# Input projection by a seven-product 2x2 block scheme, in two passes over the tokens

## The chip, the cores and the metric

One core of one Trainium2 chip runs the whole program. The metric is device time in microseconds (us) for one execution. All tensors are 32-bit floats. TensorE multiplies a stationary operand (128x128, loaded just before) by a moving operand of up to 512 columns and adds into PSUM; VectorE (DVE), ScalarE (ACT) and GpSimd (POOL) do the rest, and DMA queues are fed from SP and ACT.

## The reference

One layer of an encoder trunk. `x` is 2048 tokens by 1024 features, `w_in` is 1024 by 4616, `mem` is 256 memory tokens.

```python
h = rmsnorm(x, norm_g)
proj = h @ w_in
qk_raw, v, o, z_a, gates, u, z_b, qc, z_c = jnp.split(proj, _OFFS, axis=-1)
# widths 1024, 512, 512, 512, 8, 512, 512, 512, 512
y_a = mlstm_branch(qk_raw, v, o, ig, fg, ...) * silu(z_a)   # conv of 4 taps + silu on qk, then chunked recurrence
y_b = pool_branch(u, pool_w, pool_scale) * silu(z_b)        # causal means over 2, 4, 8, 16 tokens
y_c = mem_attn_branch(qc, mem, ...) * silu(z_c)             # softmax attention to 256 memory tokens
x = x + concatenate([y_a, y_b, y_c]) @ w_out
return rmsnorm(x, final_norm_g)
```

## The kernel before

Every large product is made from a high part and a low part of each operand (`hi` is the value rounded to the matmul's input format, `lo` the rest), and `mm3` issues three matmuls: hi by hi, hi by lo, lo by hi. The high part is made by an ACT copy, the low part by a subtraction on DVE or POOL.

**Input.** `load_x` reads the transposed `x` in four blocks of 512 tokens and eight slices of 128 features, multiplies by the norm's gain, splits into high and low (`x` tiles, one for each block and slice, all resident), and adds up squares on POOL (`acc`). The row norm is not applied to `x`: its factor (`rt`, broadcast as `rbc`) is applied to each product when it is taken out of PSUM. So the first products start before any norm is known.

**Projection, channel layout.** For a tile of 128 channels and a block of 512 tokens, `proj` issues 8 slices by 3 matmuls with the weights stationary and 512 token columns moving. There are 24 such channel tiles: 8 for q and k (`evac_qk` takes each out, applies the four-tap convolution by one ACT and three DVE instructions, then silu, then stores to `d_qk`), 4 for `zc`, 4 for `qc`, 4 for `zb` and 4 for `u`. The `u` weights are first multiplied by the pooling matrix (`pool_w`, the matmuls of L478).

**Projection, token layout.** v, o, z_a and the gates are made with the `x` tiles stationary and 256 weight columns moving (264 in the one group that holds the eight gate columns): 6 groups by 16 token tiles by 8 slices by 3 matmuls. Results go to `d_tok`. The memory's keys and values are made in the same stage and stay in SBUF.

**Order.** q and k; token layout with `gate_stats`; attention, head by head (`attend`: scores, softmax, transposes, product with values); pooling; then the last stage, in which each chunk of 128 tokens runs the recurrence (`cell`) and the output projection (`out_k`, 12 slices by 3 by 2 matmuls of 512 columns). The steps of `attend` are queued by `later(n, fn)` and run by `tick()` between projections. The output weights are prepared during the last pooling products (`prep_wo`).

A scheduler that works ahead of time orders the instructions of every engine by program order among those it holds to be ready, and sets the waits. Tile pools hand their space on: a tile of a later pool waits for the earlier tiles at its address.

## Time and profile before

| | |
|---|---|
| Runs, us | 1280.02, 1276.82, 1281.62 (median 1280.02) |
| Span of the profiled execution | 1275.6 us |
| TensorE matmul busy | 1243.3 us (97%) |
| TensorE weight load busy | 1086.5 us (85%) |
| VectorE busy | 582.6 us (46%) |
| ScalarE busy | 399.4 us (31%) |
| GpSimd busy | 247.6 us (19%) |
| DMA | 124.52 MB, mean 98 GB/s |

The span runs from the first to the last instruction of one profiled execution; what lies around it is the difference to the runs (4.4 us to the median). Matmuls overlap each other in the array, so "busy" counts time with at least one in flight, and the distance from one start to the next tells the rate. PE is the matmul, PEld its weight load.

### The profile page before, as it was taken

The numbers are of one execution on the slowest core, as the hardware profiler recorded it, in microseconds if no ns is written. First come the engines' busy times: TensorE is split into PE (matmuls) and PEld (weight loads), VectorE is DVE, ScalarE is ACT, GpSimd is POOL, SyncE is SP. The second block draws the span as 40 slices with busy tenths as digits, with TensorE's granted clock in tenths as the row PEclk, the third lists the DMA queues.
The fourth block names the chain that finished last, engine by engine and source line by source line (L and its number), as shares of the span: only waits on it lengthen the run. The fifth ranks groups of instructions, "written<-read, shape, count | busy, mean of one in ns | idle before, by whom it ended". The sixth has DMA issues, their size and how long they took to land. (4 is left out here: it accounts for less than half of the span.)

```text
span 1275.6 us, 17705 instructions
## 1 busy us (share of the span) xinstructions
PE 1243.3 (97%) x7063; PEld 1086.5 (85%) x7063; DVE 582.6 (46%) x1123; ACT 399.4 (31%) x832; POOL 247.6 (19%) x202
## 2 busy tenths in 40 slices
PE   6889999999999999999999999999989999999997
PEld 5667888999999999888888888888878888888886
DVE  6987766223300000163636354235445665656434
ACT  6744333223331221152535240100244222222212
POOL 4633000000000010000000004212434332323110
PEclk9999999999999999999999999999989999999999
DMA  6423323133311221011111012111496545454511
GB/s 208 137 62 108 100 67 104 63 102 106 96 61 67 79 70 56 26 33 33 34 33 42 25 30 62 43 49 49 158 291 236 172 150 174 149 183 140 184 57 66
DMA packets 87202, 124.52 MB, mean 98 GB/s; under 512 B 6352, under 2 KB 60880, under 8 KB 87120
## 3 DMA queue, kind: packets, MB, share of 16 engines
q1 hardware_dynamic: 56400, 102.42, 24.7%
q10 hardware_dynamic: 30720, 20.98, 5.2%
q8 instruction: 55, 0.90, 0.3%
q14 instruction: 27, 0.22, 0.0%
HBM read 85.56 MB, written 37.81 MB: 97 GB/s over the span
## 5 line engine op out<-in xcount | busy, mean ns | idle before, releaser
L147 PE MATMUL mm<-x,whi 128*128 128x512 f32 x720 | 283.9, 395 | 10.1 <-ACT x L214 7.1
L148 PE MATMUL mm<-x,whi 128*128 128x512 f32 x720 | 282.1, 392 | 2.4 <-DVE x L215 2.4
L149 PE MATMUL mm<-x,wlo 128*128 128x512 f32 x720 | 282.5, 392 | 0.0
L147 PE MATMUL mm<-whi,x 128*128 128x256 f32 (+1 forms) x768 | 217.8, 284 | 0.0
L149 PE MATMUL mm<-whi,x 128*128 128x256 f32 (+1 forms) x768 | 217.1, 283 | 0.0
L148 PE MATMUL mm<-wlo,x 128*128 128x256 f32 (+1 forms) x768 | 216.9, 282 | 0.0
L147 PEld LDWEIGHTS mm<-x,whi 128*128 128x128 f32 x720 | 136.1, 189 | 38.9 <-ACT x L214 7.1
L138 POOL TENSOR_TENSOR wlo<-wraw,whi 128x1024 fp32r<-128x1024 f32 (+1 forms) x23 | 55.7, 2421 | 557.8 <-ACT whi L137 492.1
L148 PEld LDWEIGHTS mm<-x,whi 128*128 128x128 f32 x720 | 136.0, 189 | 32.0 <-DVE x L215 3.8
L149 PEld LDWEIGHTS mm<-x,wlo 128*128 128x128 f32 x720 | 135.8, 189 | 29.0 <-issue 0.2
L147 PEld LDWEIGHTS mm<-whi,x 128*128 128x128 f32 x768 | 146.2, 190 | 0.4
L148 PEld LDWEIGHTS mm<-wlo,x 128*128 128x128 f32 x768 | 146.2, 190 | 0.2
L149 PEld LDWEIGHTS mm<-whi,x 128*128 128x128 f32 x768 | 146.0, 190 | 0.0
L442 ACT ACTIVATE tev<-mm,rt 128x256 f32<-128x256 f32 x96 | 45.4, 474 | 169.9 <-PE mm L149 168.8
L198 DVE SCALAR_TENSOR_TENSOR cacc<-text,col,cacc 128x512 f32<-128x512 f32 x96 | 82.1, 874 | 11.5 <-ACT cacc L196 10.1
L618 PE MATMUL mm<-woh,ybh 128*128 128x512 f32 x192 | 73.1, 404 | 0.0
L618 PE MATMUL mm<-wol,ybh 128*128 128x512 f32 x192 | 72.0, 398 | 0.0
L618 PE MATMUL mm<-woh,ybl 128*128 128x512 f32 x192 | 70.0, 393 | 0.0
L502 DVE TENSOR_TENSOR zc<-mm,rbc 128x512 f32<-128x512 f32 x16 | 11.0, 690 | 121.0 <-PE mm L149 121.0
L137 ACT ACTIVATE whi<-wraw 128x1024 fp32r<-128x1024 f32 (+1 forms) x37 | 39.3, 1062 | 81.5 <-PE mm L148 35.7
L774 DVE SCALAR_TENSOR_TENSOR hh<-hh,ss,gz 128x128 f32<-128x128 f32 x64 | 50.0, 841 | 30.4 <-POOL ss L772 30.4
L138 DVE TENSOR_TENSOR wlo<-wraw,whi 128x1024 fp32r<-128x1024 f32 (+1 forms) x14 | 17.2, 1228 | 94.0 <-ACT whi L137 94.0
(245 smaller groups left out, 1974.1 us busy)
## 6 DMA issues: line engine op xcount, KB each, us to landing
d_t<-tev ACTq DMA_DIRECT2D x96, 128.0 KB, 1.7
wraw<-in_wch_dram SPq DMA_DIRECT2D x17, 512.0 KB, 3.6
xr<-in_xT_dram SPq DMA_DIRECT2D x32, 256.0 KB, 3.4
d_qk<-cacc ACTq DMA_DIRECT2D x32, 256.0 KB, 2.6
d_y<-y SPq DMA_DIRECT2D x32, 256.0 KB, 2.6
yr<-d_y SPq DMA_DIRECT2D x16, 512.0 KB, 4.6
qk<-d_qk SPq DMA_DIRECT2D x16, 512.0 KB, 4.0
gz<-d_t SPq DMA_DIRECT2D x16, 512.0 KB, 3.8
```

The costliest lines, as they stand in the source:

```text
L137: A.activation(hi, raw, AF.Copy)
L138: lo_eng.tensor_tensor(lo, raw, r32(hi), ALU.subtract)
L147: T.matmul(po, ah, bh, start=first, stop=False)
L148: T.matmul(po, ah, bl, start=False, stop=False)
L149: T.matmul(po, al, bh, start=False, stop=last)
L198: V.scalar_tensor_tensor(c, t[:, i:i + BW], w(i), c, ALU.mult, ALU.add)
L442: A.activation(ev, pp[:, :256], (AF.Copy, AF.Sigmoid, AF.Silu)[n // 2], scale=rt[:, t:t + 1])
L502: V.tensor_tensor(z, pp, rbc[:, blk(b)], ALU.mult)
L618: T.matmul(outs[c][n], l, w[:, n * 512:(n + 1) * 512], start=i == 0 and p_ == 0, stop=i == KO - 1 and p_ == 2)
L774: V.scalar_tensor_tensor(hh[:, h], hh[:, h], ss[:, h:h + 1], gz[:, 1, h], ALU.mult, ALU.mult)
```

## The change

The product of tokens by features by channels is cut in two along each of the three, and the eight block products become seven by additions before and after (four sums of the token blocks S1 to S4, four of the weight blocks T1 to T3 and N4, seven additions of results). Token halves are two blocks of 512, feature halves four slices each, channel halves two tiles of 128 (or two groups of 256 in token layout). One such "quad" makes two channel tiles for 1024 tokens, or 512 token-layout columns for 1024 tokens. All 1024 tokens' seven forms of `x` fill the space that all of `x` filled before, so the kernel makes two passes `s` over halves of the tokens, and every weight is loaded and split in each pass.

The sums must be of normalised rows, so rows are normalised before the split. In the first pass squares are summed before anything else (`load_y_raw`, `norm_cols`, `scale_y`); for the second, `row_norms` squares whole rows during the first pass. Memory keys and values are made at the very start and kept in DRAM (`d_km`, `d_vm`). The eight gate columns get products of their own (`gates`). The order is: tok0, tok1, gates, 4 q/k quads, 4 attention quads, 4 pooling quads, tok2 (during which the second pass's forms replace the first's, one by one), then tok0, tok1, tok2, gates, `gate_stats`, q/k, attention, pooling, and the last stage as before. The preparation of output weights stands behind the last pooling quad.

```diff
+CH_ORDER = (("A11", "B11", "P", True), ("S2", "T2", "U", True), ("A12", "B21", "P", False),
+            ("S1", "T1", "V", True), ("S3", "T3", "W", True), ("S4", "B22", "V", False), ("A22", "N4", "W", False))
+TOK_ORDER = (("A11", "B11", "P", True), ("A12", "B21", "P", False), ("S2", "T2", "U", True),
+             ("S1", "T1", "V", True), ("S3", "T3", "W", True), ("S4", "B22", "V", False), ("A22", "N4", "W", False))
...
-            return ps.tile(list(shape), F32, name=tag, tag=tag, bufs={"mm": 3, "pv": 1}.get(tag, 2))
+            return ps.tile(list(shape), F32, name=tag, tag=tag, bufs={"mm": 4}.get(tag, 2))
...
+        def load_y_raw(s, y, i, sq=None):
...
+                    dma(y[i][h][k], xT[4 * h + k, :, b * BW:(b + 1) * BW])
...
+                            A.activation(q, y[i][h][k], AF.Square)
+                            G.tensor_tensor(acc[:, i], acc[:, i], q, ALU.add)
+        def scale_y(s, y, i):
+            b = 2 * s + i
+            rb = bcast(rt[:, 4 * b:4 * b + 4], 4)
...
+                    V.scalar_tensor_tensor(y[i][h][k], y[i][h][k], g, rb, ALU.mult, ALU.mult)
+        def x_split(f, srcs):
+            fi = FORMS.index(f)
...
+                t = xp.tile([P, 2, BW], F32R, name=f"x{f}_{k}", tag=f"x{4 * fi + k}")
+                A.activation(t[:, 0], srcs[k], AF.Copy)
+                lo_engine(3).tensor_tensor(t[:, 1], srcs[k], r32(t[:, 0]), ALU.subtract)
+        def x_steps(y):
...
+            def each(out, x0, x1, op):
+                for k in range(4):
+                    G.tensor_tensor(out[k], x0[k], x1[k], op)
+            return {
+                "A11": lambda: x_split("A11", a),
+                "A12": lambda: x_split("A12", b_),
+                "pre": lambda: each(e, c, d, ALU.add),
+                "S2": lambda: (each(c, a, c, ALU.subtract), each(a, e, a, ALU.subtract), x_split("S2", a)),
+                "S1": lambda: x_split("S1", e),
+                "S3": lambda: x_split("S3", c),
+                "S4": lambda: (each(b_, b_, a, ALU.subtract), x_split("S4", b_)),
+                "A22": lambda: x_split("A22", d),
+            }
+        NWF = 8
...
+            def prep(self, f):
+                B = self.raw
+                share = {"qk": 2, "tok": 3}.get(self.kind, 2)
+                if f == "T2":
+                    G.tensor_tensor(B["B11"], B["B12"], B["B11"], ALU.subtract)
+                    B["T1"] = B["B11"]
...
+                    G.tensor_tensor(t2, B["B22"], B["T1"], ALU.subtract)
...
+                if f == "T3":
+                    G.tensor_tensor(B["B12"], B["B22"], B["B12"], ALU.subtract)
...
+                if f == "N4":
+                    G.tensor_tensor(B["B21"], B["B21"], B["T2"], ALU.subtract)
...
+                    t = wb.tile([P, 2, 4, P], F32R, name="wf", tag="wf", bufs=NWF)
+                    A.activation(t[:, 0], src, AF.Copy)
+                    lo_engine(share).tensor_tensor(t[:, 1], src, r32(t[:, 0]), ALU.subtract)
+        def run_ch(q, d11, d12, d21, d22, done):
...
+            for n, (xfm, wfm, acc, opens) in enumerate(q.order):
+                if opens:
+                    banks[acc] = bank([P, BW], "mm")
+                pp = banks[acc]
+                for k in range(4):
+                    wh, wl = q.forms[wfm][k]
+                    mm3(pp, wh, wl, xf[xfm][k][:, 0], xf[xfm][k][:, 1], opens and k == 0, k == 3)
+                if n == 0:
+                    s1 = ev("s1")
+                    A.activation(s1, pp, AF.Copy)
+                elif n == 1:
+                    u2 = ev("u2")
+                    V.tensor_tensor(u2, pp, s1, ALU.add)
...
+        def run_tok(q, step=None):
...
+                for bk in range(2):
+                    pp = banks[acc][bk]
+                    for r in range(2):
+                        sl = slice((2 * bk + r) * P, (2 * bk + r + 1) * P)
+                        for k in range(4):
+                            mm3(pp[:, r], xt[:, 0, sl], xt[:, 1, sl], wh, wl, opens and k == 0 and r == 0, k == 3,
+                                pin=opens and k == 0 and r == 1)
...
+        def gates(s):
...
+                for k in range(4):
+                    w = wt[:, (k0 + k) * 16:(k0 + k) * 16 + P]
+                    T.matmul(pp, w, xf[f][k][:, 0], start=first and k == 0, stop=False, skip_group_check=True)
+                    T.matmul(pp, w, xf[f][k][:, 1], start=False, stop=last and k == 3, skip_group_check=True)
+            prod(g1, "A11", wgp, 0, True, True)
+            prod(g2, "S3", wgn, 0, True, False)
+            prod(g1, "A12", wgp, 4, False, True)
+            prod(g2, "A22", wgp, 4, False, True)
...
+        def conv(q):
+            s = q.s
+            ts = [misc([P, 3 + 2 * BW], "text", bufs=3) for _ in range(2)]
...
+                for i in (2, 1, 0):
+                    V.scalar_tensor_tensor(c, t[:, i:i + 2 * BW], w(i), c, ALU.mult, ALU.add)
...
+        y = make_y(1)
+        load_y_raw(1, y, 0)
+        load_y_raw(1, y, 1)
+        xs = x_steps(y)
...
+        run_tok(next(it), turn)
...
+        close(wcm)
+        fcm, fp = pool("fp")
...
+        for i in range(8):
+            prep_wo(i)
+        ybs[0] = load_y(0)
```

In `load_y_raw` the blocks `a`, `b_`, `c`, `d` of `x_steps` are token half 0 with feature halves 0 and 1, then token half 1 with feature halves 0 and 1.

## Rows read from the trace of the kernel before

**Rows 1.** The profile's page, its first lines: span, and busy time by engine.

```profile
span 1275.6 us, 17705 instructions
...
PE 1243.3 (97%) x7063; PEld 1086.5 (85%) x7063; DVE 582.6 (46%) x1123; ACT 399.4 (31%) x832; POOL 247.6 (19%) x202
```

**Rows 2.** TensorE matmuls by line and shape: count | busy us, mean ns of one | idle before.

```profile
L147 PE MATMUL mm<-x,whi 128*128 128x512 f32 x720 | 283.9, 395 | 10.1 <-ACT x L214 7.1 <-DVE text L192 2.9
...
L147 PE MATMUL mm<-whi,x 128*128 128x256 f32 x640 | 181.5, 284 | 0.0
...
L147 PE MATMUL mm<-whi,x 128*128 128x264 f32 x128 | 36.3, 284 | 0.0
...
L147 PE MATMUL pt<-x,whi 128*128 128x512 f32 x32 | 13.2, 414 | 0.0
...
L478 PE MATMUL aux<-pwr,wraw 128*128 128x128 f32 x64 | 8.4, 274 | 0.0
...
L147 PE MATMUL pv<-x,whi 128*128 128x512 f32 x16 | 6.4, 399 | 0.0
```

**Rows 3.** TensorE's timeline at 800 us: start us, duration us, what.

```profile
800.66 0.39 PE L147 MATMUL mm<-x,whi 128*128 128x512 f32 x1
...
805.19 0.39 PE L149 MATMUL mm<-x,wlo 128*128 128x512 f32 x1
805.42 1.05 PE L478 MATMUL aux<-pwr,wraw 128*128 128x128 f32 x8
806.23 0.48 PE L147 MATMUL mm<-x,whi 128*128 128x512 f32 x1
```

**Rows 4.** TensorE's timeline at 400 us, in the token-layout stage.

```profile
399.78 0.28 PE L147 MATMUL mm<-whi,x 128*128 128x256 f32 x1
...
402.99 0.28 PE L147 MATMUL mm<-whi,x 128*128 128x256 f32 x1
```

**Rows 5.** TensorE's timeline: first matmul of the program, and of the token-layout stage.

```profile
7.13 0.79 PE L147 MATMUL mm<-x,whi 128*128 128x512 f32 x1 [7.13 <-ACT x L214]
...
210.88 0.28 PE L147 MATMUL mm<-whi,x 128*128 128x256 f32 x1
```

**Rows 6.** Busy time of each engine in three stretches, then granted clock, DMA share, GB/s.

```profile
128.00:160.00 32.00, 32.00 (x143) 26.50 (x142) 25.51 (x47) 11.51 (x16) 2.39 (x1) 1.00 0.34 99
544.00:576.00 32.00, 32.00 (x177) 27.83 (x176) 22.70 (x52) 17.95 (x44) 2.38 (x1) 1.00 0.11 33
944.00:952.00 8.00, 6.74 (x25) 5.94 (x26) 1.29 (x2) 3.21 (x6) 4.68 (x3) 0.59 1.01 318
```

**Rows 7.** VectorE's timeline in the pooling stage.

```profile
787.90 1.58 DVE L510 TENSOR_TENSOR y<-p,zb 128x512 f32<-128x512 f32 x1
...
793.21 0.68 DVE L510 TENSOR_TENSOR y<-p,zb 128x512 f32<-128x512 f32 x1
```

**Rows 8.** GpSimd's timeline in the same stretch.

```profile
787.88 1.06 POOL L642 TENSOR_TENSOR usum<-uext 128x526 f32<-128x526 f32 x1
```

**Rows 9.** VectorE instructions by line and shape.

```profile
L583 DVE TENSOR_TENSOR tl<-pt,th 128x512 fp32r<-128x512 f32 x32 | 22.0, 687 | 10.0 <-ACT th L582 10.0
...
L820 DVE SCALAR_TENSOR_TENSOR xo<-xo,fs,gfb 128x1024 f32<-128x1024 f32 x15 | 20.1, 1340 | 10.2 <-POOL fs L813 10.2
```

**Rows 10.** GpSimd instructions by line and shape.

```profile
L138 POOL TENSOR_TENSOR wlo<-wraw,whi 128x1024 fp32r<-128x1024 f32 x22 | 53.2, 2418 | 516.2 <-ACT whi L137 450.4 <-PE mm L149 65.8
L221 POOL TENSOR_TENSOR acc<-acc,sq 128x512 f32<-128x512 f32 x28 | 40.4, 1443 | 28.4 <-ACT sq L220 22.0 <-ACT acc L217 5.3 <-DMA wraw<-in_wch_dram 0.3
...
L642 POOL TENSOR_TENSOR usum<-usum 128x512 f32<-128x512 f32 x4 | 4.2, 1040 | 2.8 <-DVE usum L642 2.8
```

**Rows 11.** GpSimd's timeline at the start of the program.

```profile
9.33 1.32 POOL L221 TENSOR_TENSOR acc<-acc,sq 128x512 f32<-128x512 f32 x1 [7.68 <-ACT sq L220]
...
38.63 1.47 POOL L154 TENSOR_TENSOR rt<-ms,mhalf 128x4 f32<-128x4 f32 x1 [0.70 <-DVE ms L153]
```

**Rows 12.** The DMA queues between 8 and 16 us: packets and bytes.

```profile
DMA packets 1475, 2.68 MB, mean 335 GB/s; under 512 B 297, under 2 KB 297, under 8 KB 1475
```

More of the change, by code (lines that the diff above doesn't have):

```diff
@@ L141, in load_w, with xslot @@
[L141 to L149 removed]
+        def xslot(i, shape, name, dtype=F32):
+            return xp.tile(shape, dtype, name=name, tag=f"x{i}")
@@ L151, in rsqrt_mean, with mm3 @@
+        def mm3(po, ah, al, bh, bl, first, last, pin=False):
+            ins = T.matmul(po, ah, bh, start=first, stop=False, skip_group_check=True)
+            if pin:
+                tc.keep_in_program_order(ins)
+            T.matmul(po, ah, bl, start=False, stop=False, skip_group_check=True)
+            T.matmul(po, al, bh, start=False, stop=last, skip_group_check=True)
         def rsqrt_mean(dst, src, w, n):
@@ new lines, in hybrid_block, with load_upto @@
+        quads = []
+        for s in range(2):
+            seq = [("tok", 0), ("tok", 1)]
+            rest = [(n, i) for n in ("qk", "att") for i in range(4)] + [("pool", i) for i in (3, 2, 1, 0)]
+            seq = seq + rest + [("tok", 2)] if s == 0 else seq + [("tok", 2)] + rest
+            quads += [Quad(n, s, i) for n, i in seq]
+        stream = [(q, f[1]) for q in quads for f in q.order]
+        state = {"next": 0, "used": 0, "loaded": 0}
+        def load_upto(q):
+            while state["loaded"] <= quads.index(q):
+                quads[state["loaded"]].load()
+                state["loaded"] += 1
@@ new lines, in pump, with used @@
+        def pump():
+            while state["next"] < len(stream):
+                q, f = stream[state["next"]]
+                if state["used"] + q.cost > NWF:
+                    return
+                load_upto(q)
+                q.prep(f)
+                state["used"] += q.cost
+                state["next"] += 1
+                n = quads.index(q) + 1
+                if n < len(quads) and f == ("N4" if q.tok else "T3"):
+                    load_upto(quads[n])
+        def used(q):
+            state["used"] -= q.cost
+            pump()
@@ L358, in gate_stats, with row_norms @@
+        def row_norms(t):
+            xr = misc([P, D], "xnr")
+            dma(xr, xn[t * P:(t + 1) * P])
+            A.activation(xr, xr, AF.Square, accum_out=ssq[:, t:t + 1])
+        for i in range(4):
+            conv(next(it))
+            for t in (2 * i, 2 * i + 1):
+                row_norms(8 + t)
+        rsqrt_mean(rt[:, 8:16], ssq[:, 8:16], 8, D)
+        tick()
+        close(mcm)
         def gate_stats():
@@ new lines, in attention_stage @@
+        def attention_stage():
+            mcm, pools["m"] = pool("m2")
+            set_evac(1, 1, 1)
+            ks = {}
+            kmhl = misc([P, 2, H, NMEM], "kmhl", F32R)
+            vmhl = misc([P, 2, MT, GW], "vmhl", F32R)
+            dma(r32(kmhl), d_km)
+            dma(r32(vmhl), d_vm)
+            kv["kmh"], kv["kml"], kv["vmh"], kv["vml"] = kmhl[:, 0], kmhl[:, 1], vmhl[:, 0], vmhl[:, 1]
+            for _ in range(4):
+                attention(next(it))
+            flush()
+            close(mcm)
@@ new lines, in pooling_stage, with turn @@
+        def pooling_stage():
+            mcm, pools["m"] = pool("m3")
+            set_evac(2, 2, 1)
+            for _ in range(4):
+                pooling(next(it))
+            flush()
+            close(mcm)
+        kv = {}
+        attention_stage()
+        pooling_stage()
+        mcm, pools["m"] = pool("m4")
+        set_evac(2, 2, 2)
+        y = make_y(1)
+        load_y_raw(1, y, 0)
+        load_y_raw(1, y, 1)
+        xs = x_steps(y)
+        old = dict(xf)
+        new = {}
+        def turn(n):
+            if n == 0:
+                scale_y(1, y, 0)
+                scale_y(1, y, 1)
+                xs["pre"]()
+            else:
+                f = TOK_ORDER[n - 1][0]
+                xf.clear()
+                xs[f]()
+                new.update(xf)
+                xf.clear()
+                xf.update(old)
@@ new lines, in hybrid_block @@
+        run_tok(next(it), turn)
+        xs["A22"]()
+        new["A22"] = xf["A22"]
+        xf.update(new)
+        run_tok(next(it))
+        flush()
+        close(mcm)
+        mcm, pools["m"] = pool("m5")
+        set_evac(2, 2, 4)
+        run_tok(next(it))
+        later(2, gates(1))
+        run_tok(next(it))
+        gate_stats()
+        for _ in range(4):
+            conv(next(it))
+        flush()
+        close(mcm)
+        attention_stage()
+        pooling_stage()
+        close(wcm)
@@ L838, in hybrid_block @@
             if c + 1 < NT:
-                outs[c + 1] = [bank([P, 512], "pv" if n and c % 2 == 0 else "mm") for n in range(2)]
+                outs[c + 1] = [bank([P, 512], "mm") for n in range(2)]
                 for i in range(8):
@@ L860, in hybrid_block @@
         close(scm)
+        close(fcm)
         close(xcm)
```

770 lines of the change are left out of this document (397 added, 373 removed).

## Prediction

> **What bounds the kernel now.** I read the page's head first: matmuls are in flight 1243.3 of 1275.6 us, while DVE, ACT and POOL are busy 46, 31 and 19% [rows 1]. A busy PE need not be PE at its peak, so I looked next at its timeline for the distance between starts. In the channel layout 20 steps take 805.19 - 800.66 = 4.53 us, 0.2265 us a matmul [rows 3]; in the token layout 27 steps take 402.99 - 399.78 = 3.21 us, 0.1189 us [rows 4]. The reader should see that these are steady and that no wait stands between them: time is the number of matmuls by these two prices, plus what is lost at the start and at the change to the last stage. The start: the first matmul is at 7.13 us and the token stage begins at 210.88 [rows 5]. In between lie 768 projection matmuls, 174.0 us, and about 8 us of small ones for the norms (an estimate: four broadcasts and four column sums, about 1 us each), so 210.9 - 182 = 29 us are lost. At the change to the last stage PE idles and its granted clock falls to 0.59 in the stretch 944 to 952 us [rows 6].
>
> **What it removes.** The line L147 is the first of `mm3`'s three matmuls. It has 720 + 32 + 16 = 768 entries of 512 columns and 640 + 128 = 768 in token layout [rows 2], so 2304 matmuls of each kind. After: 12 channel quads by 2 passes by 7 products by 4 slices by 3 = 2016, and 3 token quads by 2 by 7 by 16 by 3 = 2016. That is 288 fewer of each: -288 x 0.2265 = -65.2 us and -288 x 0.1189 = -34.2 us.
>
> **What it adds on TensorE.** Gates: 32 matmuls of 512 columns a pass, 64 x 0.2265 = +14.5 us, which before were 8 extra columns of 128 triples with the mean of the 256-wide ones, 284 ns [rows 2]. Turning the gates to token rows takes 8 small products a pass (two blocks of four token tiles), each issued as two instructions as those of L478 are: 32 in all, at that line's step (806.23 - 805.42)/8 = 0.10 us [rows 3], +3.2. The `u` weights are multiplied once more: 64 more of L478 [rows 2], +6.4. Norm sums, broadcasts, memory keys and values stay in number. Net on PE: -65.2 - 34.2 + 14.5 + 3.2 + 6.4 = **-75.3 us**.
>
> **Work that moves to the other engines.** Here I chose what to believe. Each channel quad now has seven weight forms to split (seven ACT copies, seven subtractions, half on DVE and half on POOL) and four weight sums on POOL: 7.5 POOL instructions of 512 columns. DVE gets five additions out of PSUM, 3.5 subtractions and, for q/k, six convolution steps of 1024 columns. With 0.69 and 1.34 us [rows 9] that is 8.5 x 0.69 + 6 x 1.34 = 13.9 us, against 84 x 0.2265 = 19.0 us of PE. Alone it fits. But DVE and POOL get in each other's way: a two-source DVE instruction took 0.68 us alone and 1.58 us beside one POOL instruction of 1.06 us that began 20 ns earlier [rows 7, 8]: 0.90 us for each meeting. If all 7.5 meet, a q/k quad costs DVE 13.9 + 6.7 = 20.6 us, 1.6 more than PE; if they fall on the additions out of PSUM, nothing. Eight such quads: 0 to +13; I take **+6**, nearer the middle because just over half of DVE's work there has two sources in SBUF.
>
> The Trainium skill has a rule that speaks against this change ("SBUF — State Buffer", section "Who interferes with whom"): a DVE instruction with two SBUF inputs and a GpSimd instruction that reads SBUF exclude each other, and the second waits for all of the first. The rows agree that it waits, at 0.90 us of 1.06; by the rule's letter the sum would be some 10 us longer.
>
> Attention quads are longer on PE by two `attend`s, and DVE was busy 22.7 of 32 us in the densest attention stretch and 25.5 of 32 in q/k [rows 6]; with the lighter evacuation I leave attention and pooling at nothing, covered by PE. If that cover is gone in pooling too, see the slow rival. ACT has 12 us in a quad of 19, and the second reading of the weights (some 18 MB, with 4 MB for `row_norms`) spreads over a millisecond on SP, with 335 GB/s reached before [rows 12], and hides behind a quad's 19 us of products: nothing; bare, each 0.5 MB weight tile would cost 1.6 us. Stores stay on ACT's queue, in as many bytes.
>
> **The start.** Now the first projection matmul needs the norm, and that hangs on POOL. The first square sum came at 9.33 us [rows 11]; with data from about 8 us POOL does 7 half-size memory sums (7 x 0.72), two memory-weight subtractions (2 x 2.42), 14 square sums (14 x 1.44) [rows 10] and one power (1.47) [rows 11]: 8 + 5.0 + 4.8 + 20.2 + 1.5 = 39.5 us, because the sums of the second block stand ahead of the power in the program. Broadcast, four scalings and a split add some 6: first token matmul at 46 us, 11.4 us of memory keys before it. Data is no limit (3.7 MB wanted first; 335 GB/s [rows 12]). The third form, S2, needs on POOL after that power: two memory subtractions 4.8, T1 and T2 4.8, a third of 16 subtractions 6.4, a power 1.5, two value-weight subtractions 4.8 and twelve token sums at half of 2.42, 14.4: 36.7 us, so with its split it is there at 78. PE has two forms (11.4 us) and half of the values (5.4) and is through at 63: 15 us lost. Five forms of 5.7 and the rest of the values then end tok0 at 112 us. Work inside: 40.0 + 11.4 + 10.9 + 4.5 = 66.8, so 45 us are lost where 29 were: **+16**. Bounds: 0, if the power goes ahead of the second block's sums (12.5 us sooner) and the lookahead fills a little more; +30, if POOL needs 1.44 instead of 1.2 a sum after the power too (+7) and eight DVE subtractions in the chain meet it (+7).
>
> **The turn.** During tok2 of pass 0 (40.0 us) POOL has to make the second pass's forms. The `y` loads (4.2 MB, 12.5 us at 335 GB/s) wait for the last pooling sums to give up their space, about 8 us; scaling brings it to 28; nine and a half us of the preparation of weights, 4.8 and 9.6 us of token sums end at 52, and S2 is split at 54, wanted at 40.0 + 11.4 = 51.4. I take **+4**; 0 if POOL is ahead, +20 if these loads queue behind the last stores on SP for 10 us and sums take 1.44. What is late next is S4, with 11 us more to spare.
>
> **The rest.** Six other pool changes: the one at 210.88 costs nothing between start and start [rows 5]; **+3** (0 to 15: an attention tail of up to 14 us before pooling gets its space, twice, half filled with the next products). A little slower matmul steps while DVE is busy, 143 starts in 32 us against 141 at 0.2265 [rows 6], so none there; **+2** for denser stretches (0 to 7). The last stage: weights may load during the last quad, whose own weight work is done by then, and POOL is free; `d_y` of the first chunk is long written. SP's last stores are passed by loads that are ready, so **0**; -5 if the dip at 944 us [rows 6] goes, +8 if eight preparations (2.42 us each on POOL for four) stand bare.
>
> **Sum.** -75.3 + 6 + 16 + 4 + 3 + 2 = -44.3 us. The profiled execution has 1275.6 + 4.4 to the median of the runs, 1280.0; so 1231.3 span, **1236 us**.
>
> **Rivals.**
> - *PE keeps all of it.* For: PE at 97%, others under half [rows 1]. Against: the chain at the start. Everything at its lower bound save 3 us: 1280 - 75.3 + 3 = 1208. Chance 0.14.
> - *DVE and POOL bound the q/k stage.* Each POOL instruction takes its full duration from DVE, 1.25 us halfway between 1.06 [rows 8] and 1.44 [rows 10]: 13.9 + 9.4 = 23.3 against 19.0, +4.3 for eight quads = 34 in place of 6: 1264. The skill's SBUF page, "Who interferes with whom", is this mechanism to the letter. Chance 0.17.
> - *Slower.* The same lock, at POOL's 1.44, in q/k and in pooling. A q/k quad is then 13.9 + 10.8 = 24.7 (+5.7); a pooling quad has DVE 9.9, weight work 10.8 and sums 1.5 x 2.42 = 3.6 on POOL, 24.3 against 19.0 + 1.6 on PE (+3.7): 75 over the 16 quads in place of 6: 1305. It decides from 3.1 us a quad. Against: 0.90 a meeting, measured, and additions out of PSUM that need no second port. Chance 0.07.
> - *My forecast*, own range 1216 to 1256: 0.62.
>
> The count of matmuls is fixed by the program, so "it does not do what it says" is no case here. About 0.5%, 6.4 us, is what a measurement can tell from no change. Faster takes the first two cases above, the forecast, less a few hundredths on the upper flank: 0.87; within 0.5% 0.06; slower 0.07. The range 1210 to 1266 leaves out half of the clean case, the flank of the lock case and the slow one.
>
> **What would show it.** 2016 matmuls of 512 columns from the quads and 2016 of 256, at 0.2265 and 0.119; a first token matmul at 33 to 55 us and a wait before S2 with POOL as its releaser; DVE at 75 to 100% in q/k stretches with PE still in flight; POOL near 550 us in all. Wrong would be: steps longer than 0.235 in quads, PE waiting on DVE's additions for more than 2 us a quad, or idle PE at the pool changes above 15 us in sum.

## The result, and the profile after

The changed kernel takes **1353.95 us** (median of four runs, 1352.35 to 1354.85) against 1278.72 us (four runs of the kernel before beside it, 1276.82 to 1281.62): a ratio of 1.0584, 95% interval 1.0565 to 1.0603. The forecast was 1236 us, with a chance of 0.07 for slower. The sign was wrong.

The head of the page of the changed kernel (span, then busy time by engine) answers to [rows 1]:

```profile
span 1351.7 us, 17582 instructions
...
PE 1207.9 (89%) x6631; PEld 1035.6 (77%) x6631; DVE 822.4 (61%) x1228; ACT 540.4 (40%) x1062; POOL 658.4 (49%) x433
```

TensorE is in flight 89% of the span instead of 97%. Its timeline in a channel quad and in a token quad (start, duration, what) answers to [rows 3, 4]:

```profile
301.62 0.39 PE L157 MATMUL mm<-xA,wf 128*128 128x512 f32 x1
...
305.97 0.39 PE L158 MATMUL mm<-xS,wf 128*128 128x512 f32 x1
...
149.85 0.28 PE L154 MATMUL mm<-wf,xA 128*128 128x256 f32 x1
...
152.91 0.28 PE L154 MATMUL pt<-wf,xS 128*128 128x256 f32 x1
```

19 steps in 4.35 us are 0.2289 us each, 27 steps in 3.06 us are 0.1133: the steps are what they were to a few per cent, longer for 512 columns and shorter for 256. So the work of TensorE can be counted as before: every matmul entry of the trace at 0.2265 us (512 columns), 0.1189 us (256 or 264) or 0.10 us (fewer). Before that is 1211.7 us, after it is 1134.8: 77.0 us less work. What a stretch has beyond this count I call lost, be it a wait or a slower step (products in full 32-bit format, most of them at the start, take longer than this count has it, so a few us of a start's loss are their work): 63.8 us before and 217.0 us after. **153.1 us more are lost where 77.0 were saved**, which is the 76.1 us between the two spans. The loss by place, an entry being put where it starts (before, the start up to 128 us lost 31.3 and the way into the last stage, 928 to 1024 us, 11.6, all else 20.9; in the changed kernel all places that the table leaves out lost 22.1):

| Lost us at | changed | e1 | e2 | e4 | e7 |
|---|---|---|---|---|---|
| start, to 128 us | 70.0 | 69.9 | 66.9 | 47.9 | 70.0 |
| q/k to attention, 256 to 304 | 10.2 | 6.1 | 6.8 | 10.6 | 9.5 |
| attention to pooling, 352 to 432 | 26.4 | 15.0 | 26.4 | 26.1 | 27.6 |
| turn, 464 to 592 | 19.3 | 23.1 | 5.4 | 18.2 | 18.8 |
| q/k to attention, 736 to 800 | 13.8 | 4.4 | 7.7 | 13.5 | 13.1 |
| attention to pooling, 832 to 928 | 26.4 | 20.6 | 25.8 | 26.8 | 25.5 |
| into the last stage, 944 to 1040 | 28.8 | 27.0 | 23.9 | 27.7 | 23.2 |

(e1 to e7 are the first experiments below.) Two stretches of quads and four of these places, in the view of busy time by stretch (PE, PEld, DVE, ACT, POOL busy, granted clock, DMA share, GB/s), answer to [rows 6]:

```profile
224.00:256.00 32.00, 31.71 (x138) 25.71 (x139) 28.67 (x32) 14.69 (x20) 20.91 (x11) 1.00 0.42 132
304.00:336.00 32.00, 32.00 (x159) 26.89 (x158) 23.21 (x42) 17.68 (x38) 14.66 (x11) 1.00 0.11 34
...
272.00:288.00 16.00, 8.49 (x29) 6.52 (x28) 11.03 (x10) 5.92 (x10) 7.32 (x5) 0.79 0.34 113
...
400.00:416.00 16.00, 12.56 (x46) 10.18 (x47) 8.21 (x17) 4.86 (x14) 3.81 (x5) 0.61 0.06 16
...
544.00:576.00 32.00, 23.40 (x142) 22.09 (x142) 23.55 (x14) 11.66 (x21) 30.70 (x18) 0.79 0.21 68
...
992.00:1008.00 16.00, 10.88 (x33) 8.00 (x34) 6.16 (x5) 5.71 (x8) 5.27 (x7) 0.66 0.83 283
```

Inside q/k TensorE is in flight 31.71 of 32 us although DVE is busy 28.67. From 400 to 416 us no engine is full (TensorE has entries in flight for 12.56 of 16 us, the next, DVE, is busy 8.21), which is how a chain of dependent steps with little beside it looks; at the turn POOL is full. A granted clock of 1.00 is the level of 2.4 GHz; after idle time the rows show 0.61 to 0.79, so a part of these stretches ran at 1.2 GHz, and that too is in the loss: in the changed kernel 212 entries of 256 and 512 columns stand at about twice the usual distance (0.21 and 0.43 us) from the next, in the stretches that the trace's records of the clock put at 0.5 or ahead of its first record. What they took beyond the count is 28 us of the 217.0; before, 28 such entries took 4.5 of 63.8. So, as an estimate from these distances, about 24 of the 153.1 us are the clock's, behind idle time that something else had made.

**The start.** POOL's timeline answers to [rows 11]:

```profile
19.47 1.72 POOL L207 TENSOR_TENSOR sqa<-sqa,sqt 128x512 f32<-128x512 f32 x1
21.15 2.80 POOL L290 TENSOR_TENSOR wr<-wr 128x1024 f32<-128x1024 f32 x1
...
27.04 2.33 POOL L293 TENSOR_TENSOR wt<-wr 128x1024 f32<-128x1024 f32 x1
29.34 2.36 POOL L296 TENSOR_TENSOR wr<-wr 128x1024 f32<-128x1024 f32 x1
...
34.00 1.74 POOL L207 TENSOR_TENSOR sqa<-sqa,sqt 128x512 f32<-128x512 f32 x1
35.70 2.83 POOL L299 TENSOR_TENSOR wr<-wr,wt 128x1024 f32<-128x1024 f32 x1
...
53.36 1.03 POOL L163 TENSOR_TENSOR rt<-ms,mhalf 128x4 f32<-128x4 f32 x1
```

On TensorE's timeline the first token product [rows 5] is:

```profile
62.80 0.29 PE L154 MATMUL mm<-wf,xA 128*128 128x256 f32 x1
```

The four weight sums of the first quad stand between the square sums; the power is done at 54.4 us (predicted 39.5) and the first token product comes at 62.8 (46). A power for each block stands on POOL's timeline, this one behind nine of the fourteen square sums and the other at 70.55 us.

**The changes of stage.** TensorE's timeline, its waits alone (in brackets the idle time before and what ended it):

```profile
281.85 0.79 PE L154 MATMUL mm<-xA,wf 128*128 128x512 f32 x1 [7.51 <-ACT s L359]
398.74 1.12 PE L739 MATMUL pt<-ident,pe 128*128 128x128 f32 x4 [3.50 <-DVE pe L730]
408.88 1.05 PE L739 MATMUL pt<-ident,pe 128*128 128x128 f32 x4 [2.20 <-DVE pe L730]
419.33 0.79 PE L154 MATMUL mm<-xA,wf 128*128 128x512 f32 x1 [2.93 <-ACT s L359]
565.59 0.50 PE L157 MATMUL pt<-wf,xS 128*128 128x256 f32 x2 [3.48 <-POOL wf L308]
775.26 0.79 PE L154 MATMUL mm<-xA,wf 128*128 128x512 f32 x1 [9.81 <-ACT s L359]
```

Behind the first of them stand, on DVE's timeline and then on ACT's:

```profile
272.34 5.91 DVE L608 SCALAR_TENSOR_TENSOR cacc<-text,col,cacc 128x1024 f32<-128x1024 f32 x3
```

```profile
278.29 1.06 ACT L609 ACTIVATE cacc<-cacc 128x1024 f32<-128x1024 f32 x1 [2.94 <-DVE cacc L608]
...
281.22 0.58 ACT L359 ACTIVATE s<-mm 128x512 f32<-128x512 f32 x1
```

The product at 281.85 adds to the bank that the first evacuation of the attention stage, `s1`, must read before. That evacuation needs a tile in the space that the last convolution of q/k gives up only after its three steps on DVE, its silu and its store (read from the order on these timelines; e1 tests it). At 398 to 419 us the transposes of the last `attend`s wait for their softmax, and the pooling stage is kept out in the same way.

**The way into the last stage.** SP's queue (an entry's duration is the time it stood):

```profile
965.86 10.09 SPq L802 DMA_DIRECT2D d_y<-zb  x4
976.01 1.22 SPq L891 DMA_DIRECT2D woraw<-in_wo_dram  x2
...
993.47 1.21 SPq L802 DMA_DIRECT2D d_y<-zb  x2
994.78 1.16 SPq L891 DMA_DIRECT2D woraw<-in_wo_dram  x2
```

The output weights come two at a time, and the third and fourth go out behind the last store of pooling.

### The profile page after: what moved, and what is told of

Read it like the earlier page. It is cut to its first block, busy times and chain, and to the rows that moved or that the text cites. A ratio compares the mean times of both kernels' runs of the same rounds, so it can differ in the third digit from the quotient of the medians.

```text
span 1351.7 us, 17582 instructions
## 1 busy us (share of the span) xinstructions
PE 1207.9 (89%) x6631; PEld 1035.6 (77%) x6631; DVE 822.4 (61%) x1228; ACT 540.4 (40%) x1062; POOL 658.4 (49%) x433
## 5 line engine op out<-in xcount | busy, mean ns | idle before, releaser
L313 POOL TENSOR_TENSOR wf<-wr,wf 128x512 fp32r<-128x512 f32 x72 | 110.8, 1541 | 204.1 <-ACT wf L312 199.7
L154 PE MATMUL mm<-xS,wf 128*128 128x512 f32 x384 | 151.9, 396 | 2.6 <-DVE z L374 2.6
L158 PE MATMUL mm<-xS,wf 128*128 128x512 f32 x384 | 150.8, 393 | 0.0
L157 PE MATMUL mm<-xS,wf 128*128 128x512 f32 x384 | 150.6, 392 | 0.0
L154 PE MATMUL mm<-xA,wf 128*128 128x512 f32 x288 | 118.3, 411 | 28.4 <-ACT s L359 23.4
L312 ACT ACTIVATE wf<-wr 128x512 fp32r<-128x512 f32 x144 | 87.6, 625 | 78.9 <-PE mm L158 63.1
L157 PE MATMUL mm<-xA,wf 128*128 128x512 f32 x288 | 116.2, 403 | 0.0
L158 PE MATMUL mm<-xA,wf 128*128 128x512 f32 x288 | 114.5, 404 | 0.0
L923 PE MATMUL mm<-woh,ybh 128*128 128x512 f32 x256 | 96.8, 417 | 5.4 <-ACT woh L895 3.7
L290 POOL TENSOR_TENSOR wr<-wr 128x512 f32<-128x512 f32 (+1 forms) x30 | 53.2, 1775 | 99.2 <-DVE wf L313 86.0
L313 DVE TENSOR_TENSOR wf<-wr,wf 128x512 fp32r<-128x512 f32 x72 | 73.5, 1022 | 36.4 <-ACT wf L312 35.9
L154 PEld LDWEIGHTS mm<-xA,wf 128*128 128x128 f32 x288 | 56.3, 196 | 43.5 <-ACT s L359 24.6
L608 DVE SCALAR_TENSOR_TENSOR cacc<-text,col,cacc 128x1024 f32<-128x1024 f32 x48 | 82.3, 1725 | 7.9 <-ACT cacc L606 7.7
L154 PEld LDWEIGHTS mm<-xS,wf 128*128 128x128 f32 x384 | 72.3, 188 | 18.8 <-DVE z L374 3.1
L157 PEld LDWEIGHTS mm<-xS,wf 128*128 128x128 f32 x384 | 72.3, 188 | 15.4
L158 PEld LDWEIGHTS mm<-xS,wf 128*128 128x128 f32 x384 | 72.1, 188 | 15.3
L308 DVE TENSOR_TENSOR wf<-wr,wf 128x512 fp32r<-128x512 f32 x46 | 51.6, 1137 | 31.5 <-ACT wf L307 26.8
L307 ACT ACTIVATE wf<-wr 128x512 fp32r<-128x512 f32 x72 | 44.3, 627 | 61.7 <-PE pt L158 34.8
L308 POOL TENSOR_TENSOR wf<-wr,wf 128x512 fp32r<-128x512 f32 x26 | 39.1, 1507 | 59.2 <-ACT wf L307 53.3
```

What stands on the lines that cost most here:

```text
L154: ins = T.matmul(po, ah, bh, start=first, stop=False, skip_group_check=True)
L157: T.matmul(po, ah, bl, start=False, stop=False, skip_group_check=True)
L158: T.matmul(po, al, bh, start=False, stop=last, skip_group_check=True)
L290: G.tensor_tensor(B["B11"], B["B12"], B["B11"], ALU.subtract)
L307: A.activation(t[:, 0], src[:, 2 * kk:2 * kk + 2], AF.Copy)
L308: lo_engine(share).tensor_tensor(t[:, 1], src[:, 2 * kk:2 * kk + 2], r32(t[:, 0]), ALU.subtract)
```

## The experiments

Theory S says that a change of stage loses what the old stage's tail keeps from the new one: its space, and work to stand beside the tail. Theory L, the rival, says that DVE and POOL, loaded and in each other's way, make everything late. Every run is one time beside a run of the kernel before on the same chip (1278.6 to 1280.8 us), unless an interval is given. Five times of one kernel, e11, spread over 9.5 us, so a few us between single runs say little alone; the losses by place say more.

**e1: evacuation tiles that stay.**

```diff
+        ecm, ep = pool("ep")
-            return misc(list(shape), name, dtype, tag=tag, bufs=pools[tag])
+            if name in ("s1", "u2"):
+                return ep.tile(list(shape), dtype, name=name, tag=name, bufs=2)
+            return misc(list(shape), name, dtype, tag="e", bufs=pools["e"])
```

> The changed kernel (1354 us) with one edit: the evacuation tiles s1 and u2, two of each, live in a pool of their own that stays open over all stages, so that the first evacuations of a stage don't wait for the space of the stage before; the attention keeps its second query in u2. Theory S (the pools' hand-on of space stops TensorE at each change of stage): the four changes q/k to attention and attention to pooling lost 74 us by the sum of matmul pitches (9.9, 13, 25.5, 25.3); with s1 and u2 free TensorE can go six steps of 2.7 us into the new stage instead of being stopped by the first evacuation, so about 8 us each come back, and the time is 1310 to 1330 us. Rival L (POOL's sums and subtractions make every chain late, the space is only where it shows): the new stage starts a few steps earlier and stands just as long further on; 1345 to 1358 us.

1324.82 us, 29 less. S holds, and by place too (table): 4.1, 11.4, 9.4 and 5.8 us come back at the four changes, while the turn loses 3.8 more. What is left at attention to pooling is put down to the chain itself; e9 tests that.

**e2: no weight sums.**

```diff
-                    G.tensor_tensor(B["B11"], B["B12"], B["B11"], ALU.subtract)
-                    G.tensor_tensor(t2, B["B22"], B["T1"], ALU.subtract)
-                    G.tensor_tensor(B["B12"], B["B22"], B["B12"], ALU.subtract)
-                    G.tensor_tensor(B["B21"], B["B21"], B["T2"], ALU.subtract)
```

> The changed kernel without its weight sums: the four subtractions on POOL that make T1, T2, T3 and N4 in each quad of products are left out and the raw blocks stand in their place (the output is not the reference's). All steps of TensorE stay, POOL loses 120 operations of about 1.6 us (some 190 of its 658 us). Theory L: POOL is what makes the start, the turn and the ends of the stages late; of the 150 us that the changed kernel loses beyond the one before, 60 us or more come back, 1260 to 1295 us. Theory S: only the start (the first sums stand ahead of the square sums) and a part of the turn come back, 1325 to 1340 us, and the losses at the four inner changes of stage stay within 5 us each of what they were.

1320.97 us: 33 less, between the two ranges and 4 us from S's. By place it is neither alone. The turn gives back 13.9 us, the two changes out of q/k 3.4 and 6.1 (as it would be if their last convolution were quicker with POOL free, which no run shows apart), the last stage 4.9; attention to pooling gives nothing (26.4 and 25.8). So POOL's load is the turn, and a part of three other places; it is not the attention's end. At the start the first token product came 14 us earlier, at 48.8 us, and the last product of the first quad only 3.1 us earlier (136.4 for 139.5): other POOL work, the forms of x, then held its later steps (5.87 us of waiting before one of them, at 110.9 us).

**e3: token quads between the stages.** Kept tiles as in e1, and:

```diff
-            seq = [("tok", 0), ("tok", 1)]
+            seq = [("tok", 0)] + qk + [("tok", 1)] + att + mid + pl + ([] if s else [("tok", 2)])
```

> The changed kernel with the evacuation tiles s1, u2 and e in a pool that stays open, and the quads in another order: in the first pass the second token quad stands between q/k and attention, in the second pass the second token quad stands between q/k and attention and the third between attention and pooling (pe has two buffers instead of three). Theory S: a token quad (38 us of steps that need only the kept tiles) covers three of the four inner changes, whose losses of 9.9, 13 and 25.3 us go to under 4 each; the fourth (25.5) falls by some 8 as in the run with kept tiles alone; start, turn and the way into the last stage stay; 1300 to 1315 us. Theory L: the covered changes lose their stands but the steps of the token quads are stretched instead by the engines that are late; 1335 to 1355 us.

1335.53 us, which is L's number, but not by L's cause. The covered places fell to -0.2, 1.2 and 0.7 us, as S said; but 16.6 us were lost at 800 to 864 us, ahead of the token quad meant to cover the attention's end, 10.1 and 10.4 in the two q/k stages that now follow the gates at once (128 to 256 and 592 to 720 us), and the turn rose to 27.8. Waits there:

```profile
224.73 0.79 PE L155 MATMUL mm<-xS,wf 128*128 128x512 f32 x1 [4.34 <-DVE s L371]
...
846.24 0.70 PE L741 MATMUL pt<-ident,pe 128*128 128x128 f32 x4 [2.21 <-DVE pe L732]
```

The transposes wait for the softmax with a whole token quad ready behind them: TensorE takes its queue in order. What made DVE late in the q/k stages stays open.

**e4: square sums on TensorE.**

```diff
-                            G.tensor_tensor(acc[:, i], acc[:, i], q, ALU.add)
+                        for t in range(4):
+                            T.matmul(rowsum[i][:, t:t + 1], q[:, t * P:(t + 1) * P], ones[:, 0:1],
+                                     start=kk == 0 and t == 0, stop=kk == 7, skip_group_check=True)
```

> The changed kernel with the square sums of the first two token blocks taken from POOL: TensorE adds the eight squared tiles of a block up in a bank by 32 products with a column of ones, in place of 14 additions on POOL (1.0 to 1.7 us each) and the product behind them. Theory L for the start (the first token product stood at 62.8 us because the square sums came behind weight sums in POOL's order): the first token product comes at about 48 us and the loss up to 128 us falls from 69 to about 52; 1336 to 1342 us. Rival (the start is held by the chain of norms, scaling and sums on DVE and by the loads): the first product moves by under 5 us; 1348 to 1356 us.

1337.72 us, 16 less; the first token product at 50.5 us (62.8), and 47.9 us lost up to 128 us (70.0), against which TensorE has 11.2 us more to do by the count. L for the start holds.

**e5: every tail beside a token quad.** Kept tiles; pooling before attention; token quads behind the attention in both passes; the second pass's loads, scaling and half of its x sums beside the first of two at the turn; the first eight output weights loaded into the block weights' buffers.

```diff
+            body = qk + [("pool", i) for i in (3, 2, 1, 0)] + att
+            seq = [("tok", 0)] + body + [("tok", 1), ("tok", 2)] if s == 0 else [("tok", 0), ("tok", 1)] + body + [("tok", 2)]
...
+                "pre": lambda: (each(e, c, d, ALU.add), each(c, a, c, ALU.subtract)),
+                "S2": lambda: (each(a, e, a, ALU.subtract), x_split("S2", a)),
...
+            if i < 8:
+                raw = wb.tile([P, D], F32, name="woraw", tag="wr", bufs=4)
```

> The changed kernel with kept tiles s1, u2 and e, and every stage's end laid beside quads that don't need its space: each pass runs q/k, pooling, attention (not q/k, attention, pooling); in the first pass the second and third token quads follow the attention, and the loads, scaling and half of the x sums of the second pass run beside the second one; in the second pass the third token quad follows the attention, and the first eight output weights are loaded into buffers of the block weights and split beside it. Theory S (what is lost at a change of stage is the tail of the old stage with nothing beside it; by the sum of matmul pitches after the run with kept tiles loses 14 and 20 us at attention to pooling, 17 to 24 at the turn, 26 into the last stage, of 166 us up to 1040 us): attention's tails are covered (under 5 us left each), the turn goes to 5 to 10, the way into the last stage to 8 to 14, 6 us come anew at q/k to pooling in place of q/k to attention; 1265 to 1285 us. Theory L (DVE and POOL are what is short there): the turn and the last stage keep their losses; 1295 to 1315 us.

1288.97 us: 65 less than the changed kernel, 4 above S's range and 6 below L's. Of its changes only two were also run alone, the kept tiles (e1) and the output weights (e7). **e6** is e5 with e4's square sums.

> The kernel e5_order with the square sums of the first two blocks on TensorE (as in e4_pe_squares, which took 16 us off the start). The start and the rest don't meet, so by both theories the two gains add: 14 to 18 us below e5_order, 1248 to 1270 us by theory S, 1278 to 1300 by L. If it stays above the kernel before (1280), what is left of the losses is to be looked for in the first 130 us and in the turn.

1275.48 us, 13.5 below e5, just short of the 14 to 18 that both theories gave; the time itself lies between their ranges. The losses of these and the later runs:

| Lost us at | e5 | e6 | e8 | e9 | e10 |
|---|---|---|---|---|---|
| start, to 128 us | 71.4 | 48.0 | 50.1 | 51.9 | 49.9 |
| first attention's end, 400 to 448 | 14.2 | 14.7 | 14.9 | 1.1 | 15.1 |
| turn, 448 to 592 | 6.1 | 3.2 | 6.1 | 10.4 | 16.2 |
| second attention's end, 864 to 928 | 18.4 | 20.1 | 18.3 | 9.3 | 19.4 |
| into the last stage, 928 to 992 | 9.1 | 7.2 | 9.5 | 4.7 | 9.8 |

The turn (19.3 in the changed kernel) and the way into the last stage (28.8) come down as S said. The attention's two ends do not: a token quad stands beside them and 14.2 and 18.4 us are still lost in e5.

**e7: output weights loaded early**, in the changed kernel, by the last edit of e5 alone.

> The changed kernel with one edit at its end: the first eight output weights are loaded into the four buffers of the block weights, which are free some 20 us before the last quad ends, in place of two buffers whose space is free only after it; their splits still need the space of the last quad's forms. Theory Q (the way into the last stage lost 27 us because the loads of the output weights stood in SP's queue behind the last stores of y, and two buffers let only two through at a time): 10 to 18 us come back, 1335 to 1344 us. Rival (the splits on ACT, DVE and POOL, 2 to 3 us each beside each other, are what TensorE waits for): under 4 us, 1350 to 1356 us.

1346.17 us, 7.8 less, between Q and its rival. The first loads now go out at 939.9, 943.5 and 961.4 us (976.0 in the changed kernel), but the place still loses 23.2 of 28.8 us. The loads were a part; most of the rest came back only in e5, where a token quad follows instead of pooling.

**e9: the attention's products held to the written order**, on top of **e8**, which is e6 with its square sums in the rounded format (four entries a tile in place of eight).

```diff
-        tmp = xslot(16, [P, 2, BW], "sqt")
+        tmp = xslot(16, [P, 2, BW], "sqt", F32R)
+        ones_r = const([P, 2], "ones_r", F32R)
```

> The kernel e6_order_sq with the squared tiles and the column of ones in the rounded format of the projections, so that a product of the square sums is one pass (the four of a tile took 1.85 us in e6_order_sq, 30 us of TensorE from 12 to 46 us; the products of 256 columns in the rounded format take 0.12 us each). Theory L for the start (whatever engine makes the square sums holds the first token product): the first token product comes at 36 to 42 us instead of 50.5, the loss up to 128 us falls from 46 to about 35, 1263 to 1269 us. Rival (the loads and POOL's weight sums hold it): the first product moves by under 4 us, 1272 to 1277 us.

1282.51 us: 7 us *more* than e6 and outside both ranges. Yet the first token product came at 44.7 us (50.5) and the last product of the first quad 2.7 us earlier. But the mean step of 512 columns from 130 to 400 us (of all below 0.35 us) is 0.2347 us where e6 had 0.2306, and it is longer in the stages behind too; see e11.

The edit of e9 holds these products behind what is written before them on TensorE, and moves them apart:

```diff
+                        if m == 0 and i == 0:
+                            tc.keep_in_program_order(ins)
-            later(3, lambda: transposes(0))
-            later(4, lambda: transposes(1))
-            later(5, pv)
+            later(4, lambda: transposes(0))
+            later(5, lambda: transposes(1))
+            later(7, pv)
```

> The kernel e8_r_squares with the attention's own products (scores, transposes, sums over memory) held to their place in the written order on TensorE, and the transposes one tick later and the sums over memory two ticks later than before. In e6_order_sq the two ends of the attention still lost 14 and 24 us, in waits of 0.8 to 2.9 us of the transposes for the softmax. Theory O (the order of TensorE's queue was laid out for shorter durations of DVE and ACT than the chip's, so the queue stands at products that come too early): 12 to 25 us below e8_r_squares. Rival S (the attention's last chain is simply long and the token quad beside it is stopped by its two banks of the other ring): within 5 us of e8_r_squares.

1261.82 us, 20.7 below e8: theory O. The two ends go from 14.9 to 1.1 and from 18.3 to 9.3 us; 4 us of it is lost again at the turn. The pins and the later steps were not run apart. The attention's last transposes now stand earlier, from 413.8 us (427.1 in e8). Stretches 400 to 432 us of e8 and, below, of e9:

```profile
400.00:416.00 16.00, 13.72 (x108) 12.95 (x106) 10.26 (x26) 14.43 (x27) 1.86 (x2) 1.00 0.48 148
416.00:432.00 16.00, 10.27 (x47) 7.81 (x48) 10.18 (x24) 6.15 (x18) 0.00 (x0) 0.83 0.23 67
```

```profile
400.00:416.00 16.00, 15.58 (x120) 14.73 (x119) 9.56 (x22) 13.17 (x27) 1.29 (x1) 1.00 0.27 77
416.00:432.00 16.00, 16.00 (x132) 15.73 (x131) 8.27 (x15) 5.25 (x9) 3.49 (x3) 1.00 0.37 118
```

**e10: every second x sum on DVE**, on top of e8.

```diff
-                    G.tensor_tensor(out[k], x0[k], x1[k], op)
+                    (V if k % 2 else G).tensor_tensor(out[k], x0[k], x1[k], op)
```

> The kernel e8_r_squares with every second x sum on DVE instead of POOL (16 of the 32 sums). Theory P (POOL alone is short where the forms of x are made: at the start TensorE waited 6.1 us for a low of S3 on POOL): 4 to 8 us below e8_r_squares. Theory L (DVE and POOL beside each other take turns: 1.75 and 1.71 us an operation at 105 to 121 us of the changed kernel, 0.68 and about 1.05 alone, so moved work costs the other engine the same): within 2 us of e8_r_squares.

1297.78 us, 15 *more*. Both theories missed: TensorE now waited for DVE at the start, and at the turn the loss rose from 6.1 to 16.2 us with DVE busy 16.00 of 16 us (14.56 in e8). DVE, which also takes the products out of PSUM, seems to have been the shorter of the two there. TensorE's timeline, then a stretch of the turn:

```profile
80.59 0.80 PE L161 MATMUL mm<-wf,xS 128*128 128x256 f32 x2 [6.27 <-DVE xS L229]
86.70 0.58 PE L161 MATMUL mm<-wf,xS 128*128 128x256 f32 x1 [3.82 <-DVE xS L229]
```

```profile
496.00:512.00 16.00, 13.58 (x112) 13.12 (x111) 16.00 (x13) 5.64 (x11) 14.71 (x7) 1.00 0.10 34
```

**e11 and e12: where the operands stand.** The two floats of `ones_r` in e8 had moved every tile allocated behind it by 32 bytes. By the addresses of the built programs, which no view of the traces shows, the split weights and the forms of x both stood 32 bytes behind a multiple of 64 before, after and in e6; in e8 to e10 the weights and their neighbours stood at a multiple of 64 and the forms of x did not.

```diff
-        ones_r = const([P, 2], "ones_r", F32R)
+        ones_r = const([P, 16], "ones_r", F32R)
```

> The kernel e9_att_pins with the rounded column of ones sixteen columns wide instead of two (two are used), so that all tiles that are allocated behind it, the split weights among them, lie 64 bytes further on instead of 32 and stand again where they stood against blocks of 64 bytes in e6_order_sq. From e6_order_sq to e8_r_squares the mean distance of two matmuls of 512 columns rose from 0.2306 to 0.2348 us, in every stage, though neither their operands' shapes nor their order had changed, and the split weights had moved by 32 bytes against the forms of x. Theory A (the place of the weights in memory sets the distance): it falls to 0.229 to 0.232 us and the time to 1240 to 1252 us. Rival (something else of e8, denser engines or the rounded squares): the distance stays at 0.234 to 0.236 us and the time at 1258 to 1264 us.

e12 leaves `ones_r` at two columns and moves the other side instead:

```diff
+        pcm, pad = pool("pad", side="right")
+        G.memset(pad.tile([P, 8], F32, name="pad", tag="pad"), 0.0)
         xcm, xp = pool("xp", side="right")
```

> The kernel e9_att_pins with a pad of 32 bytes ahead of the tiles on the other side (the forms of x and the output weights), so that the split weights stay at the start of a block of 64 bytes, as in e9_att_pins, and the forms of x move there too (in e6_order_sq both stood 32 bytes behind one). Theory A in the form that the two must stand alike: 1240 to 1252 us at 0.229 to 0.232 us between matmuls of 512 columns. Theory A in the form that the weights' own place counts: 1258 to 1264 us at 0.234 to 0.236 us, as e9_att_pins. Rival as in e11_addr_back: both runs stay at e9_att_pins.

e11: 1249.27 us (5 runs), 0.9764 of the kernel before, 95% interval 0.9733 to 0.9795. e12: 1247.07 us (4 runs), 0.9756, interval 0.9728 to 0.9783. TensorE's timeline at 300 us of e8, and below of e11:

```profile
299.64 0.39 PE L160 MATMUL mm<-xS,wf 128*128 128x512 f32 x1
...
305.94 0.40 PE L160 MATMUL mm<-xA,wf 128*128 128x512 f32 x1
```

```profile
299.64 0.39 PE L157 MATMUL mm<-xS,wf 128*128 128x512 f32 x1
...
305.99 0.39 PE L160 MATMUL mm<-xS,wf 128*128 128x512 f32 x1
```

27 steps in 6.30 us are 0.2333 us; 28 steps in 6.35 are 0.2268. e12 has 0.2287 as its mean over 130 to 400 us, e11 0.2289, e9 0.2346. So theory A holds against its rivals: two edits that only move tiles took the step back. The form that the two must stand alike (at 32 and 32, or at 0 and 0) fits e8 to e12, but it is not all of it: e6 and the changed kernel stand at 32 and 32 too, and by the same mean they have 0.2306 and 0.2315. Both kernels beat the kernel before by 2.4%.

## Why the prediction was wrong, step by step

**Net work of TensorE, -75.3: right.** 77.0 us less by the count. The 512-column steps were longer and the 256-column ones shorter than the prices taken; by the distances shown above that is some 5 us more for 2080 of the one and 11 less for 2016 of the other (an estimate).

**The lock in the q/k stage, +6, and the rivals of 1264 and 1305: the lock came, the price did not.** Weight subtractions on DVE took 1022 ns and convolution steps 1725, against 687 and 1340 for such shapes [rows 9]. The view by line and shape (count, busy us, mean ns of one, idle before):

```profile
L608 DVE SCALAR_TENSOR_TENSOR cacc<-text,col,cacc 128x1024 f32<-128x1024 f32 x48 | 82.3, 1725 | 7.9 <-ACT cacc L606 7.7
L313 DVE TENSOR_TENSOR wf<-wr,wf 128x512 fp32r<-128x512 f32 x72 | 73.5, 1022 | 36.4 <-ACT wf L312 35.9
```

But the quads lost next to nothing inside (2.9 us from 128 to 272 us, gates and all). The cover held; the price appears where the last convolution of the stage is the chain. POOL was busy 658.4 us in all, where about 550 was forecast.

**The start, +16: mis-sized, measured +39** (70.0 against 31.3). The step that failed is the order on POOL: I let all twelve token weight sums come behind the power. Four of them, 10.3 us, and four subtractions of the memory weights in place of two stood ahead of it. I was wrong the other way as well, and lucky there: nine square sums stood ahead of the power, not fourteen. e4 shows that the square sums on POOL cost 16 us of the whole; e2 shows that the weight sums cost about 3 us of the first quad's end, and that the forms of x hold what comes next.

**Six other pool changes, +3 (0 to 15): the step that failed most.** The four changes between q/k, attention and pooling lost 77 us, where the prediction had called more than 15 us of idle time at such changes a sign that it was wrong. The bracket held "an attention tail of up to 14 us before pooling gets its space, twice, half filled with the next products". e1 shows why so little was filled: after two products the third needs the bank that only the new stage's first evacuation can free, and that evacuation waits for the old stage's space. e9 shows the other half: even with other work ready, TensorE's queue had the tail's products too early in its order. Before, there was no such place: attention and pooling shared one pool, and the change from attention to pooling lost nothing that shows in the 7.0 us between 224 and 928 us. No term stood for the clock, which falls behind such idle time.

**The turn, +4 (0 to 20): measured 19**, inside the bounds, at the far end. POOL is busy 30.70 of 32 us there, and e2 gives 13.9 back: POOL's sums and splits of 512 columns take 1.6 us there instead of 1.2.

**The last stage, 0 (-5 to +8): failed, +17** (28.8 against 11.6). I had the weights loading during the last quad; their two buffers came free too late and their loads stood behind stores (e7, 8 us), and their splits met the pooling sums (the rest, by e5, where it goes with a token quad there; these two were not separated further).

The forecast had TensorE's own work right and the time between its stretches of work wrong: 23 + 74 + 15 + 17 = 129 us too little, less 8 for the lock in q/k and the denser steps that did not come and 2 for the work, 119 us, against 118 missed.

## What to carry to other kernels

When work on the full engine shrinks, count what the engine has beside each tail of a stage, and not only the tails: a stage's first evacuation tile, its space and the order of the engine's queue decide how many products can run ahead. Look at each place where a pool closes for the first instruction that needs a new tile, and put a quad that needs none of the new space beside it, with the tail's products late enough in the queue. A faster product was worth 2.4% here only after that; 1.0% of it came with the places of the operands (e9 to e11).

## What the runs showed of the hardware that was not expected

**DVE and POOL take turns.** Where both run two-source instructions from SBUF back to back, each takes the sum of both. DVE's timeline of the changed kernel, then POOL's:

```profile
111.76 1.75 DVE L532 TENSOR_TENSOR vmhl<-vmt,vmhl 128x512 fp32r<-128x512 f32 x1
113.43 3.43 DVE L223 TENSOR_TENSOR xS<-y,xS 128x512 fp32r<-128x512 f32 x2
```

```profile
111.25 1.71 POOL L232 TENSOR_TENSOR y<-y,y 128x512 f32<-128x512 f32 x1
112.92 1.71 POOL L223 TENSOR_TENSOR xS<-y,xS 128x512 fp32r<-128x512 f32 x1
```

1.75 is 0.68 + 1.06 us [rows 7, 8]. The Trainium skill ("SBUF — State Buffer", section "Who interferes with whom") says that the two exclude each other for the whole instruction; here the trace agrees in full: 1.75 us for an instruction of 0.68 beside one of 1.06, where the meeting of [rows 7] had cost 0.90.

**The operands' places in memory change TensorE's step.** 0.2333 us in e8 against 0.2268 in e11; from e9 to e11 only places changed, and the mean went from 0.2346 to 0.2289 us. The same section of the Trainium skill ("SBUF — State Buffer", "Who interferes with whom") calls the ports for moving operands and for weight loads independent; of the operands' places it does not speak, and these runs do not show whether the ports have a part in it. Why, and whether it is the weights, the forms or their neighbours, is open. The step of 256 columns moves as well, and not the same way: 0.12 us in the kernel before, 0.113 in the changed kernel, 0.12 again in e11 and e12 (the median distance of two starts on TensorE's timeline).

**A product with one column took twice as long at the start as later.** In e6 eight entries (four products) of one column in full 32-bit format took 1.86 us, each 0.21 us behind the last, and 1.03 us, each 0.11 behind the last, 31 us later:

```profile
12.23 1.86 PE L210 MATMUL pt<-ones,sqt 128*128 128x1 f32 x8 [12.23 <-ACT sqt L206]
...
42.94 1.03 PE L210 MATMUL pt<-ones,sqa 128*128 128x1 f32 x8
```

The steps of 256 columns beside them halve at the same time, from 0.21 to 0.12 us. The trace's first record of the clock in e6 comes there, at 40.8 us, with 1.0: what stands ahead of it went at the distances of the lower level, though the views print 1.00 for that stretch too. So a price for a product is not to be read from the start of a trace.
